# Threshold attention on one core: the last of 48 head pairs taken out of the screen and computed whole in float32

## The chip, the core and the metric

The kernel runs on one core of a Trainium2 chip. The core has a matrix engine (PE, with its weight loads as a row of their own, PEld), a vector engine (DVE), a scalar engine (ACT), a general engine (POOL) and a queue engine for transfers (SP). Each engine works through its own list in order and waits on semaphores. The metric is the device time of one execution in microseconds (us); the time of a kernel is the median of its runs.

## The reference

Q, K and V have 8 batches x 12 heads, each with 512 rows of 64 floats. The threshold is 0.1.

```python
scale = 1.0 / np.sqrt(Q.shape[-1])
scores = np.einsum('bhqd,bhkd->bhqk', Q, K) * scale
weights = np.exp(scores - np.max(scores, axis=-1, keepdims=True))
weights = weights / (np.sum(weights, axis=-1, keepdims=True) + 1e-10)
weights = np.where(weights > threshold, weights, 0)
weights = weights / (np.sum(weights, axis=-1, keepdims=True) + 1e-10)
return np.einsum('bhqk,bhkd->bhqd', weights, V).astype(np.float32)
```

Most rows of random data have no weight above 0.1, and their output is zero. A row with exactly one weight above 0.1 gets that weight normalised to one, so its output is the V row of that key. The kernel relies on this: it finds the few rows that may hold such a weight, computes these exactly, and copies V rows. A check at the end branches to a slow general path if a row falls outside these cases.

## The kernel before, in words

**Tiling.** The 96 heads make 48 pairs (`hp`), two pairs make one of 24 quads (`q`, four heads), eight pairs make one of six groups (`x`). Two heads of a pair lie on the lower and the upper 64 partitions, so that their matmuls use the two row halves of PE.

**The screen, for each pair, in float16.** K is loaded (SP, `load_k`, L399), transposed on PE (`ktr`, L422) and copied out of PSUM in float32 (`kev`, into `kt`); POOL casts it to float16 (`kh`). Q is cast on POOL (`qcast`, L412), transposed (`qtr`, L433) and copied out (`qev`). Four score steps (`sc`, L468) give, for both heads, 128 keys x 512 queries each. ACT or DVE takes the exponential of each (`ex`; ACT at L476, DVE at L478 by an integer trick), and two `g` steps of eight matmuls each (L497) add up sums and high powers of them over the keys into one PSUM bank, `acc`, which holds a whole group. `bits` and `size` (L458, L504) add a bound on the norms of the rows. So `acc` is complete after the last `g` and `size` of a group, and `evac` (DVE, L507) copies it out.

**The exact rows, for each group.** After `evac` come `test` (PE, L513), `flags` (DVE, L517), `rank` (PE, L523 and L525), `key` (DVE, L529), `oh` (a one-hot array, DVE, L533), `idx` (eight matmuls on PE, L543, which turn the one-hot array into row numbers), `idxev` and `base` (DVE, L547 and L552), `gather` (POOL, an indirect DMA of up to 128 rows of Q, 16 slots for each pair, L557), `split` (POOL, L564), `xtr` (PE transpose, L569), `xev` (copy, ACT or DVE), `xqk` (PE, float32 scores of the gathered rows against `kt`, eight matmuls in 32-column tiles, L583), `xexp` (ACT, exponential with the row sum, L589), `xcut` (DVE, threshold times sum, L594), `xkeep` (DVE, which compares and adds up the number of the one key above, L598), `xvi` and `xoi` (DVE, L604 and L609), `gv` (POOL, gather of V rows, L613) and `scatter` (POOL, an indirect DMA of these rows to the output, L620). The output is set to zero beforehand by 24 stores from SP (`z`, L627). For all groups but the last this chain lies beside the screens of the next group. The chain of group 5 has nothing behind it.

**The order.** The order of all 1148 steps is written out by hand in the table `ORDER`: a token is a step's number, the letter of its engine (A, D, G, P, S) and the buffers it takes. `Plan.run` issues the steps in this order, so each engine's list is the table filtered by its letter. Steps are declared with their predecessors by `add`. Two `spare` steps issue matmuls on an idle tile into `acc` (L201): 6 behind `rank` and 17 behind `idx` of group 5. `check` steps gather the conditions for the branch at the end (L733 to L757).

In the table of before, PE's list ends: the last `g` of pairs 45, 46 and 47, with `xtr` of group 4 ahead of the last one, then `xqk` 4, `test` 5, `rank` 5, `spare` 0, `idx` 5, `spare` 1, `xtr` 5, `xqk` 5. DVE's ends: `evac` 5, `flags` 5, `xcut` 4, `xkeep` 4, `xvi` 4, `xoi` 4, `key` 5, `oh` 5, `check` 1, `idxev` 5, `base` 5, `xcut` 5, `xkeep` 5, `xvi` 5, `check` 2, `xoi` 5. POOL's ends: `gv` 4, `gather` 5, `split` 5, `scatter` 4, `gv` 5, `scatter` 5. A scatter declares the output rows from 0 to the end of its group, so the program makes it wait for every earlier write in these rows to land.

Of the kernel before, what the change touches and what calls it, by code (L numbers as in the profile page):

```python
# [13 lines left out]
12S3 13A2 7G 8G 37S 5G 11D 38S 9G 64S2 6G 0G 88S 14G1 15P0.1 1D 18A3 2G 20P2.3 19A 21D 22A 10D 3G 40P4.5  # L14
23P2.6.13 16D9 17A 4G 65S1 41D 42A 26P1.3.12 24A 25D 29P0.5.11 89S 39G 28A 32P2.4.10 27D 115S1 31A 43G 44P3.6
30D 35P 34A 45D 46A 67P1.5 33D 47P0.4.9 68A8 50P3.6.8 69A 61D2 36P 48A 70G2 49D 52A 53P1.2.7 56P0.5.6 66G0 54A
51D 62P 116S0 91P4.6 58A 55D 90G 71P1.3 156S0 92A 59P 72D 93A 73D 95P2.5 57D 94G 74P1.4.5 77P3.6.4 75A 76D 60P
96A 97D 80P0.1.3 78A 79D 83P2.4.2 82A 118P3.5 81D 85A 98P1.6.1 84D 86P 100A 157S2 119D7 87P 120A 117G1 218S3
112D1 101P0.4.0 99A 104P2.6.13 107P3.5.12 103A 102D 113P 121G1 106A 122P1.4 108D 105A 110P 109D 123A 159P0.6
124A 111P 160D6 161A 125P2.3.11 153D0 128P1.5.10 162G0 63S 127A 131P0.4.9 126D 219S1 130A 154P 134P3.6.8 129A  # L20
158G0 259S2 133D 139P2.5.7 132A 135D 137P 140A 142P1.4.6 136D 145P0.3.5 141A 147D 144A 163P2.6 138P 146A 164D
165D 221P3.4 143A 194D2 148P2.5.4 222A5 166P0.6.3 151P 150D 167A 195P 149D 223A 169P1.3.2 172P0.5.1 260S0 168A
170D 224G3 152P 173A 300S1 171D 175P2.4.0 174A 180P1.6.13 220G1 176D 182A 178P 181D 177A 183P0.3.12 186P2.5.11
184A 179P 187D 185A 225P4.6 262P0.1 188A 226D 227A 189P2.3.10 263D4 192P 190A 114S 264D 228P4.5.9 261G0 191A
155S 231P0.6.8 230D 232A 301S2 234P1.2.7 193P 236A 229D 196S 265G2 237P3.5.6 235A 341S0 197D1 242P0.2.5 233A
245P1.4.4 244D 243A 240P 238A 246D 266P2.6 247A 198P0 239D 303P1.3 267D 268A 248P4.5.3 199D 241P 304A3 256D1
254P 305A 297D0 200P 250A 306G1 251P2.6.2 201D 249A 269P1.3.1 202D1 272P0.5.0 271A 257P 298P 252D 273A 203P4
302G1 274D 270A 275P2.3.13 253A 204D2 278P0.1.12 276D 342S1 206G1 279A 307P5.6 205D 277D 258S 283P2.4.11 308A
255P 299S 309D 285A 281P 280D 403S3 284A 286P0.3.10 338D2 289P5.6.9 287A 292P1.4.8 282P 288D 293A 339P 294D 291A
295P 290A 310P0.2.7 344P1.3 312A 311D 313P4.6.6 343G0 296P 345D2 346A 314A 316P2.5.5 315D 319P0.3.4 318A 347G0  # L30
348P1.4 317D 320A 322P 321D 324P5.6.3 207G1 327P0.2.2 404S0 349D 325A 323P 328D 329A 444S2 208P3 350D 330P1.5.1
326A 333P0.2.0 209D1 332D 331A 351P3.4.13 210P6 335A 352D 334A 379D1 353A 380P 336P 211A1 337P 445S2 212D 405G1
213D 354P1.5.12 340S 406P2.3 356A 485S1 357P0.4.11 214D 215D 355A 407D1 360P5.6.10 216G2 358A 363P 408D 361A
410P1.2 359D 362A 365P0.3.9 409G3 366D 367A 368P4.5.8 364P 369A 370D 371P3.6.7 411A 374P0.4.6 372D 377P 412A
446G0 375D 376A 447P1.5 373A 413P2.3.5 441D0 381S 416P0.4.4 448A0 486S1 378P 417D 449A 451P1.6 526S0 415D 418A
419P0.5.3 450G2 414A 382D0 422P3.4.2 421A 420D 442P 424A 425P 452D 453A 427P2.5.1 423D 430P0.4.0 429A 433P1.6.13
428D 217G 383P3 432A 426P 384D 431A 482D2 385P 434A 436P2.5.12 386D 454P0.4.11 437A 387D0 443S 488P1.3 456A
# [74 lines left out]
def kernel(  # L112
# [13 lines left out]
    nc = tc.nc  # L126
    B, H, S, D = Q.shape
# [6 lines left out]
    GP = 8  # L134
# [700 lines left out]
```

## Time and profile before

| | |
|---|---|
| median of 3 runs | 184.74 us (184.69 to 185.29) |
| profiled execution, its own time | 186.93 us |
| its span | 185.2 us |
| busy share of the span: PE, DVE, ACT, POOL | 90%, 85%, 80%, 46% |
| granted PE clock, mean | 0.986 |
| DMA queue of SP (q1) | 37.50 MB, 72.1% of 16 engines' span |

The span runs from the first to the last recorded instruction or transfer. A row of the profile in order of time gives the start in us, the duration in us, the engine, the line of the kernel, the operation, the tiles written and read with their shapes, and the count of like instructions merged into the row; in brackets stands how long the engine had been idle and what released it. Rows of the chain of waits give start, duration and what the chain ran through. Busy shares are averages over the screens, where three engines are full, and the end, where they are not.

### The profile page before, as it was taken

How to read it: one execution, taken by the hardware profiler on the slowest of the kernel's cores; microseconds unless marked ns; L12 is line 12 of the kernel's file. 1: busy time of each engine (PE TensorE's matmuls, PEld its weight loads, DVE VectorE, ACT ScalarE, POOL GpSimd, SP SyncE). 2: the span in 40 equal slices, each digit the busy share in tenths (PEclk: the TensorE clock that was granted, in tenths of full speed). 3: DMA queues.
4: the chain of work that ended last, by engine and by line, in shares of the span. 5: the costliest groups of instructions: out<-in, count | busy, mean ns of one | idle time of the engine just before them, and what ended most of it. 6: DMA issues, size and time to landing. Idle time of an engine off the chain costs nothing.

```text
span 185.2 us, 5894 instructions
## 1 busy us (share of the span) xinstructions
PE 167.5 (90%) x2272; PEld 69.0 (37%) x2272; DVE 157.2 (85%) x337; ACT 148.8 (80%) x305; POOL 85.7 (46%) x130
## 2 busy tenths in 40 slices
PE   7896999999999999999999998999999999998700
PEld 2443444443343354433545334444344243334200
DVE  6897899999979979879898999999999999955040
ACT  2786999998979999989999697999979999930100
POOL 7751626365346573684441934646706504004322
PEclk9999999999999999999999999999999999999995
DMA  5996999999979999969799789999999000000000
GB/s 139 237 253 166 288 256 251 328 264 355 248 159 333 303 284 292 298 145 207 136 378 395 170 224 340 312 287 292 270 274 370 13 1 11 0 0 5 9 2 10
DMA packets 67457, 38.45 MB, mean 208 GB/s; under 512 B 51901, under 2 KB 64257, under 8 KB 67425
## 3 DMA queue, kind: packets, MB, share of 16 engines
q1 hardware_dynamic: 66576, 37.50, 72.1%
q8 instruction: 19, 0.31, 0.8%
q0 software_dynamic: 576, 0.27, 0.7%
q10 hardware_dynamic: 272, 0.26, 0.5%
q14 instruction: 14, 0.11, 0.2%
HBM read 25.56 MB, written 12.78 MB: 207 GB/s over the span
## 4 chain that ended last, share of the span: by engine, by line
PE 51%; DVE 15%; ACT 11%; issue 8%; DMA 6%; SPq 5%; POOL 1%; POOLq 0%; ACTq 0%; DVEq 0%
PE bank L468 17%; PE acc L497 16%; ACT e L476 10%; DVE e L478 6%; PE bank L583 5%; PE bank L422 5%; SPq L399 4%; DMA k<-in_K_dram 3%; PE bank L433 3%; PE acc L504 2%; DVE v L458 2%; DVE kt L390 2%; DVE oh L533 2%; PE bank L543 1%; DMA vr<-in_V_dram,idx 1%
## 5 line engine op out<-in xcount | busy, mean ns | idle before, releaser
L476 ACT ACTIVATE e<-bank 128x512 f16<-128x512 f32 x236 | 122.0, 631 | 7.6 <-PE bank L468 6.4
L478 DVE TENSOR_SCALAR e<-bank 128x512 int16<-128x512 f32 x148 | 93.6, 680 | 1.6 <-PE bank L468 1.4
L468 PE MATMUL bank<-qk 64*128 64x512 f16 x384 | 66.3, 380 | 2.6 <-DVE e L478 0.5
L497 PE MATMUL acc<-e,w_sum 128*32 128x512 f16 x384 | 56.8, 383 | 0.1
L497 PE MATMUL acc<-e,w_pow 128*32 128x512 bf16 x384 | 56.8, 384 | 0.0
L392 POOL CAST qk<-kt 128x1024 f16<-128x1024 f32 (+1 forms) x25 | 25.8, 1034 | 40.5 <-DVE kt L390 24.3
L412 POOL TENSOR_SCALAR qh<-q 128x512 f16<-128x512 f32 x48 | 32.5, 678 | 20.0 <-DMA q<-in_Q_dram 10.2
L468 PEld LDWEIGHTS <-qk 64*128 64x128 f16 x384 | 18.5, 94 | 38.4 <-issue 35.1
L497 PEld LDWEIGHTS <-w_sum 128*32 128x32 f16 x384 | 13.8, 95 | 25.7 <-issue 20.6
L422 PE MATMUL bank<-identity_f,k 64*128 64x64 f32 x384 | 17.6, 229 | 1.7 <-DMA k<-in_K_dram 1.3
L422 PEld LDWEIGHTS bank<-identity_f,k 64*128 64x128 f32 x384 | 14.6, 140 | 8.6 <-issue 3.0
L458 DVE TENSOR_SCALAR v<-qk 128x1024 int32<-128x1024 int32 x24 | 17.1, 720 | 0.7 <-ACT qk L388 0.6
L388 ACT COPY kt<-bank 128x512 f32<-128x512 f32 (+1 forms) x30 | 15.8, 567 | 0.8 <-PE bank L422 0.3
L390 DVE COPY kt<-bank 128x512 f32<-128x512 f32 (+1 forms) x22 | 14.1, 659 | 2.3 <-PE bank L422 2.1
L390 DVE COPY qk<-bank 128x512 f16<-128x512 f16 (+1 forms) x32 | 11.9, 394 | 2.5 <-PE bank L433 2.1
L497 PEld LDWEIGHTS <-w_pow 128*32 128x32 bf16 x384 | 13.8, 95 | 0.3 <-issue 0.2
L613 POOL DMA_INDIRECT vr<-in_V_dram,idx x6 | 6.5, 1081 | 13.8 <-DVE keys L529 8.8
L388 ACT COPY qk<-bank 128x512 f16<-128x512 f16 (+1 forms) x20 | 11.7, 601 | 0.7 <-PE bank L433 0.7
L583 PE MATMUL bank<-kt,xq 128*32 128x512 f32 x96 | 11.5, 598 | 0.4 <-ACT xq L388 0.4
L433 PE MATMUL bank<-identity_h,qh 64*128 64x64 f16 x384 | 10.9, 192 | 0.2
L433 PEld LDWEIGHTS <-qh 64*128 64x128 f16 x384 | 8.6, 95 | 5.9 <-issue 3.8
L201 PE MATMUL acc<-idle 128*128 128x512 f16 x32 | 9.3, 449 | 1.2 <-DVE idle L197 1.2
(94 smaller groups left out, 99.9 us busy)
## 6 DMA issues: line engine op xcount, KB each, us to landing
k<-in_K_dram SPq DMA_DIRECT2D x96, 128.0 KB, 4.8
out_dram<-zero SPq DMA_DIRECT2D x24, 512.0 KB, 6.4
q<-in_Q_dram SPq DMA_DIRECT2D x22, 512.0 KB, 5.7
q<-in_Q_dram SPq DMA_DIRECT2D x3, 256.0 KB, 3.4
q<-in_Q_dram ACTq DMA_DIRECT2D x1, 256.0 KB
qs<-in_Q_dram,idx POOLq DMA_INDIRECT x6, 5.0
vr<-in_V_dram,idx POOLq DMA_INDIRECT x6, 4.0
out_dram<-vr,idx POOLq DMA_INDIRECT x6, 3.8
```

The source lines that it names most:

```text
L388: keep(nc.scalar.copy(dst, src))
L390: keep(nc.vector.tensor_copy(dst, src))
L392: keep(nc.gpsimd.tensor_copy(dst, src))
L412: keep(nc.gpsimd.tensor_scalar(dst, src, ALPHA, 1.0, op0=ALU.mult, op1=ALU.mult))
L422: keep(nc.tensor.matmul(bank_at(("kp", u), i)[:, c:c + D], lhsT=src[ps, n0 + n, r, :], rhs=identity_f32[ps, ps], is_transpose=True, start= ...
L433: keep(nc.tensor.matmul(bank_at(("qp", u), i)[:].bitcast(f16)[:, c:c + D], lhsT=src[ps, n0 + n, r, :], rhs=identity_h[ps, ps], is_transpos ...
L458: keep(nc.vector.tensor_scalar(v_b[at("v", q)][:].rearrange("p a n c -> p (a n c)").bitcast(i32), qk_b[at("qk", q)][:].rearrange("p a n c ...
L468: keep(nc.tensor.matmul(bank_at(("sc", hp, t), h)[:], lhsT=qk[ps, 1, n, t * P:(t + 1) * P], rhs=qk[ps, 0, n, :], start=True, stop=True))
L476: keep(nc.scalar.activation(dst, src, ACTF.Exp, scale=math.log(2.0) / 1024.0, bias=exp_bias))
L478: keep(nc.vector.tensor_scalar(dst.bitcast(i16), src, EXP_BIAS * 1024.0, 0.0, op0=ALU.add, op1=ALU.max))
L497: keep(nc.tensor.matmul(acc[32 * j:32 * j + 32, :], lhsT=w, rhs=rhs, **turn(x, j)))
L583: keep(nc.tensor.matmul(bank_at(("xs", x))[32 * b:32 * b + 32, :], lhsT=xq[:, a * P + 32 * b:a * P + 32 * b + 32], rhs=kt_b[at("kt", GQ * ...
```

## The change

- Pair 47 (`DN`, the last) leaves the screen. The last quad's unit holds one pair; its `bits`, `size` and zero store take half; `acc` of group 5 gets 7 pairs; `limits_last` keeps pair 47's flags at zero; `xqk` 5 has seven matmuls.
- Pair 47 is computed whole. Its K and Q come as one more K-shaped unit (24): both are transposed in float32 and copied out by two `kev` steps. Four `dsc` steps (for 128 queries each, two heads, 512 keys in float32, in PE's two row halves) are followed by eight `dexp` (ACT, with row sum), four `dcut`, eight `dkeep` and four `dvi` (DVE), eight `dgv` (POOL, gathers of 128 V rows each into `d_rows`) and two `dst` (SP, plain stores of 128 KB each, for one head each, behind all four gathers of that head). Rows without a key above the threshold take zeros that `d_rows` was set to.
- `oh` of group 5 becomes two halves, `oh0` and `oh1`, and `idx` two halves of four matmuls, `idx0` and `idx`.
- `spare` becomes three steps of 6 matmuls (behind `rank`, `idx` and the second spare) in place of 6 and 17. A `check` 3 takes in the new pair's conditions.
- The pool of `xe` buffers has 4 in place of 2.
- `ORDER` is written anew from the first line, with 1180 steps. 227 exps of the screen go to ACT and 149 to DVE (236 and 148 before).

The new lists at the end, as the table gives them. PE: `sc` of pair 46 with `dsc` 0 ahead of its last step, `dsc` 1, 3, 2, `size` 23, `g` of 45 (second half), 46, 46, `xtr` 4, `test` 5, `xqk` 4, `rank` 5, `spare` 0, `idx0`, `idx`, `spare` 1, `spare` 2, `xtr` 5, `xqk` 5. ACT: `dexp` (t, h) 0,0, the last `ex` of pair 46, `dexp` 1,0, 1,1, 3,1, 2,0, 2,1, 0,1, 3,0, `xexp` 4, `xev` 5, `xexp` 5. DVE: the last `ex`, `bits` 23, `dcut` 1, `dkeep` 1,0 and 1,1, `dvi` 1, `evac` 5, `xev` 4, `dcut` 2, `dkeep` 2,0, `flags` 5, `dkeep` 2,1, `dvi` 2, `dcut` 0, `dkeep` 0,0, `key` 5, `dcut` 3, `oh0`, `oh1`, `xcut` 4, `check` 1, `idxev` 5, `xkeep` 4, `xoi` 4, `xvi` 4, `base` 5, `dkeep` 3,0, 0,1, `dvi` 0, `dkeep` 3,1, `check` 3, `dvi` 3, `xcut` 5, `xkeep` 5, `xvi` 5, `xoi` 5, `check` 2. POOL: `split` 4, `dgv` 1,1, 1,0, 2,0, 2,1, `gather` 5, `gv` 4, `split` 5, `dgv` 0,0, 0,1, 3,1, 3,0, `gv` 5, `scatter` 4, `scatter` 5. SP: `dst` 1, `dst` 0.

```diff
+    DN = NP - 1
...
     def load_k(u):
...
+            src = (Kf, Qf)[n][DN] if q == NQ else Kf[2 * q + n]
...
-    def do_oh(eng, x):
+    def do_oh(eng, x, cs=slice(0, C2)):
+        k = cs.stop - cs.start
...
+                if GP * x + n == DN:
+                    continue
...
+    def do_dsc(eng, t):
+        kt = kt_b[at("kt", NQ)]
+        for h in range(2):
+            ps = slice(h * D, (h + 1) * D)
+            keep(nc.tensor.matmul(bank_at(("ds", t), h)[:], lhsT=kt[ps, 1, t * P:(t + 1) * P], rhs=kt[ps, 0, :],
+                                  start=True, stop=True))
+
+    def do_dexp(eng, t, h):
+        c = 2 * t + h
+        keep(nc.scalar.activation(xe_b[at("xe", ("d", t, h))][:], bank_at(("ds", t), h)[:], ACTF.Exp, scale=scale,
+                                  accum_out=d_sums[:, c:c + 1]))
+
+    def do_dcut(eng, t):
+        keep(nc.vector.tensor_scalar(d_cuts[:, 2 * t:2 * t + 2], d_sums[:, 2 * t:2 * t + 2], thr, None, op0=ALU.mult))
+
+    def do_dkeep(eng, t, h):
+        c = 2 * t + h
+        keep(nc.vector.scalar_tensor_tensor(out=junk[:], in0=xe_b[at("xe", ("d", t, h))][:], scalar=d_cuts[:, c:c + 1],
+                                            in1=key_no[:].rearrange("p r c -> p (r c)"),
+                                            op0=ALU.is_gt, op1=ALU.mult, accum_out=d_accs[:, c:c + 1]))
...
+    def do_dgv(eng, t, h):
+        c = 2 * t + h
+        keep(nc.gpsimd.indirect_dma_start(
+            out=d_rows[:, h, t, :], out_offset=None, in_=Vr,
+            in_offset=bass.IndirectOffsetOnAxis(ap=d_idx[:, c:c + 1], axis=0),
+            element_offset=(2 * DN + h) * S * D, bounds_check=S - 1, oob_is_err=False))
+
+    def do_dst(eng, h):
+        keep(nc.sync.dma_start(out=Of[DN][:, h, :, :], in_=d_rows[:, h, :, :]))
...
-    add(("spare", 1), "PE", [("idx", last)], lambda e: spare(acc, 17))
+    for i, (n, behind) in enumerate(((6, ("rank", last)), (6, ("idx", last)), (6, ("spare", 1)))):
+        add(("spare", i), "PE", [behind], lambda e, n=n: spare(acc, n))
```

More of the change, by code (lines that the diff above doesn't have):

```diff
@@ L282 @@
     limits = consts.tile([P, 4 * COLS], f32)
+    limits_last = consts.tile([P, 4 * COLS], f32)
     tri_f = consts.tile([P, P], f32)
@@ L501, in do_size @@
         v, row = v_b[at("v", q)], 8 + 2 * m
-        for j in range(4):
+        for j in range(4) if q < NQ - 1 else (0, 2):
             w = w_size[j // 2][:, 31 - row:63 - row]
@@ L647, in free @@
             return [("bk", (name, x))]
-        sums_of = [("g", GP * x + m, half) for m in range(GP) for half in range(2)]
+        sums_of = [("g", GP * x + m, half) for m in range(GP) if GP * x + m != DN for half in range(2)]
         sums_of += [("size", GQ * x + m) for m in range(GQ)]
@@ L660, in exact @@
         stage("gather", "POOL", s("idxev"), do_gather, [("qs", x, 1)])
-        stage("split", "POOL", s("gather", "base"), do_split, [("qb", x, 1)], [("qs", x)])
+        stage("split", "POOL" if x < NX - 1 else "POOL DVE", s("gather", "base"), do_split, [("qb", x, 1)], [("qs", x)])
         stage("xtr", "PE", s("split"), do_xtr, bk("xt"), [("qb", x)])
```

237 lines of the change are left out of this document (147 added, 90 removed).

## The prediction

> **What bounds the kernel now.** I read the windows table first, then the chain of waits, then the rows in order of time behind the last screen. Columns of the windows: stretch, its length, then busy us and count for PE, weight loads, DVE, ACT and POOL, the granted clock, the DMA share.
>
> ```profile
> 140.00:150.00 10.00, 9.87 (x146) 3.67 (x147) 10.00 (x19) 9.98 (x21) 5.50 (x6) 1.00 0.35 136
> 150.00:157.00 7.00, 6.79 (x106) 3.00 (x105) 6.56 (x17) 6.70 (x14) 2.40 (x2) 1.00 0.03 7
> 157.00:163.60 6.60, 6.48 (x75) 2.15 (x76) 5.95 (x10) 5.99 (x13) 0.39 (x1) 1.00 0.00 0
> 163.60:170.00 6.40, 5.30 (x48) 2.29 (x41) 4.08 (x14) 0.69 (x2) 1.04 (x1) 1.00 0.02 4
> 170.00:178.00 8.00, 4.91 (x30) 1.54 (x28) 1.48 (x7) 0.95 (x3) 2.57 (x4) 1.00 0.02 5
> 178.00:185.20 7.20, 0.38 (x2) 0.09 (x2) 0.63 (x4) 0.00 (x0) 1.91 (x2) 0.64 0.04 8
> ```
>
> Up to 163.6 us PE, DVE and ACT are all full: 98, 90 and 91% busy in the third row. From 163.6 on they are mostly free; there the five PE figures contain idle-tile matmuls. The end is a chain of short steps:
>
> ```profile
> 163.60 0.81 DVE L507 TENSOR_SCALAR ev<-acc,root_of 128x512 int32<-128x512 int32 x1 [0.66 <-PE acc L497]
> 165.21 0.34 PE L513 MATMUL bank<-test_w,ev 128*128 128x48 bf16 x4
> 165.59 0.36 DVE L517 TENSOR_TENSOR marks<-bank,limits 128x192 bf16<-128x192 f32 x1 [1.18 <-PE bank L513]
> 166.01 0.19 PE L523 MATMUL bank<-marks,tri 128*128 128x64 bf16 x1 [0.45 <-DVE marks L517]
> 167.30 0.21 DVE L529 TENSOR_TENSOR keys<-bank,marks 128x64 bf16<-128x64 f32 x1
> 167.55 0.71 DVE L533 TENSOR_TENSOR oh<-slot_no,keys 128x1024 f16<-128x1024 bf16 x1
> 169.01 0.22 DVE L547 TENSOR_SCALAR idx<-bank,slot_add 128x1 int32<-128x1 f32 x1 [0.18 <-PE bank L543]
> 170.00 1.00 POOL L557 DMA_INDIRECT qs<-in_Q_dram,idx  x1 [1.42 <-DVE ix L552]
> 172.54 0.39 POOL L564 TENSOR_TENSOR qb<-qs,ix 128x128 f32<-128x128 f32 x1 [1.54 <-DMA qs<-in_Q_dram,idx]
> 172.99 0.33 PE L569 MATMUL bank<-identity_f,qb 128*128 128x128 f32 x1 [0.33 <-POOL qb L564]
> 177.37 0.21 DVE L604 TENSOR_SCALAR idx<-accs,ix 128x1 int32<-128x1 f32 x1
> 177.85 1.04 POOL L613 DMA_INDIRECT vr<-in_V_dram,idx  x1 [3.28 <-DVE oks L739]
> 181.15 1.02 POOL L620 DMA_INDIRECT out_dram<-vr,idx  x1 [2.26 <-DMA vr<-in_V_dram,idx]
> ```
>
> Call E the start of evac of group 5, 163.60. Then the gather of Q rows starts at E+6.40, xtr at E+9.39, the gather of V rows (gv 5) at E+14.25, scatter 5 at E+17.55, and the span ends at 185.20, 4.05 behind scatter 5. So the time is E plus 21.6 us of chain, and the change touches both.
>
> **Part 1: E.** The rows that price one step:
>
> ```profile
> 147.01 0.54 PE bank L468 x4
> 147.55 0.55 PE acc L497 x8
> 163.37 1.91 PE L583 MATMUL bank<-kt,xq 128*32 128x512 f32 x16
> 65.35 0.71 PE bank L422 x16
> 152.07 10.65 ACT L476 ACTIVATE e<-bank 128x512 f16<-128x512 f32 x21
> 158.08 4.87 DVE L478 TENSOR_SCALAR e<-bank 128x512 int16<-128x512 f32 x8
> 165.35 0.60 ACT L589 ACTIVATE xe<-bank 128x512 f32<-128x512 f32 x1 [2.04 <-PE bank L583]
> 165.84 0.19 ACT L589 ACTIVATION_READ_ACCUMULATOR xe<-bank 128x1 f32 x1
> 166.26 0.75 DVE L598 SCALAR_TENSOR_TENSOR junk<-xe,sums,key_no 128x512 bf16<-128x512 f32 x1
> 166.93 0.08 DVE L598 DVE_READ_ACCUMULATOR junk<-xe,sums,key_no 128x1 f32 x1
> 166.07 0.15 DVE L594 TENSOR_SCALAR sums<-sums 128x1 f32<-128x1 f32 x1
> 163.04 0.27 ACT L388 COPY xq<-bank 128x128 f32<-128x128 f32 x1 [0.32 <-PE bank L569]
> 4.95 0.62 POOL L412 TENSOR_SCALAR qh<-q 128x512 f16<-128x512 f32 x1
> 5.20 0.69 PE L422 MATMUL bank<-identity_f,k 64*128 64x64 f32 x8
> ```
>
> A pair's score step (two heads) is 0.27 us on PE, half a g 0.55, a float32 pass over 512 columns in one round of tiles 1.91/4 = 0.48; an exp steps at 10.65/21 = 0.51 on ACT and 4.87/8 = 0.61 on DVE; an exp with row sum 0.49 to its read plus 0.19 = 0.68; a keep 0.67 + 0.08 + a gap = 0.79, a cut or an index step 0.15 to 0.2.
>
> PE, ahead of E: pair 47 loses 4 score steps (1.08) and 2 g (1.10), half a Q transpose and half a size (0.3 together); it gains 8 float32 transposes, half of 0.71 (0.35), and four dsc, all listed ahead of the last g. The trace has no float32 matmul in 64-row tiles. If the two heads run side by side like the 64-row score steps, a dsc is two passes, 0.96, four 3.84; if they run one behind the other, 7.68; less than 3.84 is excluded, since two passes of one head can't overlap on the same rows. I take 3.84, as both tilings in the trace do overlap. Net: -2.48 + 0.35 + 3.84 = +1.7.
>
> ACT, ahead of E: the table has 227 exps for 236, -9 x 0.51 = -4.6; of the six dexp listed ahead of evac only three stand in a chain to it (dexp 0,0 ahead of the last screen exp, and 1,0 and 1,1, which feed dkeep on DVE), +2.0; copies about nought. Net -2.5.
>
> DVE, ahead of E: one exp more (+0.6), two keeps (+1.6), dcut and dvi (+0.3), five half-size K copies for two full ones and shorter Q copies (about 0), a half-size kh (+0.3), half a bits (-0.3). Net +2.5. Note dvi 1 and its keeps are queued ahead of evac: the chain dsc 1 (0.96), two dexp (1.4), dcut, two keeps, dvi (2.0) is 4.4 us behind the last score step; PE needs three dsc, size and three g, 2.9 + 0.2 + 1.65 = 4.75 for the same stretch. So PE, not this new wait, ends last.
>
> The three sums are -2.5, +2.5 and +1.7; exps can move between ACT and DVE, whose mean is 0. PE is the fullest (98%, with 0.12 us idle in 6.6), so its sum weighs most: I take **+1.3**, with -2.5 and +2.5 as ends. POOL's three more memsets (an estimate: 0.5 together) and the new order of its constants lie ahead of the first Q cast, which stood at 4.95; PE's first K transposes come at 5.20 and K's copies behind them, so up to 0.3 of a later cast is covered and I count nothing. The extra K-shaped loads of pair 47's Q replace Q loads of the same bytes, and the DMA share late is 0.03: nothing. The half zero store: nothing.
>
> **Part 2: E to gv 5.** Test now runs ahead of the exact matmuls of group 4 (before, behind them: 0.8 lost), so it ends at E+1.2. But DVE's list reads evac, xev 4, dcut, dkeep, flags: 0.75 + 0.3 (as ACT's copy of xq) + 0.2 + 0.79 puts flags at E+2.0, where it was (E+1.99). Rank now waits behind xqk 4 on PE, which waits for xev 4: E+1.1 plus 1.9 gives E+3.0 to 3.1, before E+2.41. Then dkeep, dvi, dcut, dkeep lie ahead of key: E+4.15, before E+3.70. One-hot in halves lets four of eight index matmuls lie beside the second half, worth 0.3; check 1 sits ahead of idxev. idxev E+5.95, before E+5.41: **+0.5**. POOL has four dgv ahead of this gather; at 1.04 each, the last started behind dvi 2 at E+3.5, they end at E+5.6, no wait. gv 4 (1.04) fits into the 2.5 us in which the gather lands. Behind split 5 (E+9.9) stand four dgv, to E+14.1; gv 5 would be due at E+14.75. They just fit. Ends: 0 if the gather has 0.27 us of lag (gv 5 had: index written by 177.58, start 177.85) for its 0.77 before; +1.3 if the DMA issues don't fit. Fewer spare matmuls leave PE idle about 1.5 us ahead of xtr 5; the clock was 1.00 in the window 170 to 178, with 3 us of idle PE: nothing.
>
> **Part 3: gv 5 to the end.** Scatter 4 moves from ahead of gv 5 to behind it. In the program as it was, each scatter waits for the landing of the one ahead of it, since their declared rows of out overlap; the two dst stores lie in scatter 5's rows too. So scatter 5 gets two new waits.
>
> ```profile
> 177.85 2.50 DMA vr<-in_V_dram,idx
> out_dram<-vr,idx POOLq DMA_INDIRECT x2, 2.2
> vr<-in_V_dram,idx POOLq DMA_INDIRECT x2, 2.4
> k<-in_K_dram SPq DMA_DIRECT2D x96, 128.0 KB, 4.8
> ```
>
> The first row is of the chain, two are of the DMA view from 165 us on, the last is of the page; figures are us to landing. Before: gv 5 landed 2.50 behind its start, and scatter 5 started 0.8 later, at +3.30. Now scatter 4 starts at +1.04, lands at +3.24, and with the same 0.8 scatter 5 starts at +4.05. The last dgv starts at E+13.1, lands at E+15.5; dst 0 lands 2.2 later (as a scatter) to 4.8 later (as a K load under traffic). DMA is all but idle here, so nearer the low end: 2.5, E+18.0, scatter 5 at E+18.8, the same place. **+0.75**, ends +0.75 and +3.0. A write's landing is never free to the next: the Trainium skill, DMA: Bandwidth & Descriptors, section "Anatomy of one DMA — SWDGE (gpsimd) path", puts about 2.0 us of fixed time, mostly the write's receipt, HBM's the slowest, into each DMA, plus bytes over 436 GB/s: as an estimate 2.3 us for the 128 KB of dst, and the sum would be 0.2 less on that branch and unchanged overall.
>
> **The sum.** 1.3 + 0.5 + 0.75 = +2.55. The profiled execution took 186.93 us, 185.20 of span and 1.73 around it; its median of three is 184.74, 2.19 below it. So span 187.75, and a median of 184.74 + 2.55 = **187.3**.
>
> **Rivals.**
> *ACT sets E (faster).* The exps leave ACT, and if DVE absorbs its 2.5 in its 10% of idle and PE likewise, E moves by ACT's -2.5: 184.74 - 2.5 + 1.25 = 183.5. For it: ACT ran 21 exps without a gap to 162.7. Against: PE goes on with the last g until evac at 163.60. It decides from E earlier by 1.8. Chance 0.16.
> *Half of it.* E earlier by about 1.25, given back behind: 184.7. Chance 0.13.
> *POOL becomes the queue.* Indirect DMA instructions are not all 1.04:
>
> ```profile
> 125.94 1.38 POOL L557 DMA_INDIRECT qs<-in_Q_dram,idx  x1 [2.21 <-DVE idx L547]
> 167.54 1.04 POOL L613 DMA_INDIRECT vr<-in_V_dram,idx  x1 [8.79 <-DVE keys L529]
> ```
>
> At 1.38 the four dgv behind split 5 take 1.4 more, of which 0.65 is covered: gv 5 0.8 later, dst with it: 188.1. Against: the second row ran beside the one-hot, a DVE step with two SBUF inputs, in 1.04. Chance 0.12. The Trainium skill, GPSIMD Engine Reference, section "1. Specifications", says that POOL's SBUF interfaces contend with VectorE instructions of two SBUF inputs, which the keeps are; by that rule this case is the likely one, and the second row doesn't bear it out.
> *The store is slow.* dst lands in 4.8: scatter 5 at +3.0 in place of +0.75, 189.5. Chance 0.07.
> *The two heads don't overlap in float32.* +3.84 on PE: 191.1. Chance 0.05.
> The forecast itself, 186.0 to 188.5: 0.47.
>
> From these cases: slower by over 0.3% (0.55 us, about what a measurement here tells from no change) 0.71, within 0.13, faster 0.16. The range leaves out most of the first rival below and the last above: 184.4 to 189.8.
>
> **What would show it.** Right: dsc rounds near 0.48 on PE, evac 5 near 164.9, four dgv in a row between split 5 and gv 5 with little idle, scatter 5 released by a landing of out and not of vr, about 4 us behind gv 5. Wrong: evac ahead of 162; scatter 5 still 3.3 behind gv 5; keeps that delay evac behind the last g; or a new order of the table that gains or loses microseconds in the middle, which no row here can price.

## The result, and the profile after

| | before | after |
|---|---|---|
| median beside each other | 185.01 us (184.69 to 185.66) | 191.48 us (190.06 to 191.69) |
| ratio after/before, 95% interval | | 1.033 [1.027, 1.039] |
| profiled execution, and its span | 186.93, 185.2 us | 191.46, 189.7 us |
| E, start of `evac` 5 | 163.60 | 164.87 |
| `gather` 5, `gv` 5, `scatter` 5 start | E+6.40, +14.25, +17.55 | E+6.38, +15.06, +20.66 |
| end of the span | E+21.6 | E+24.83 |

The change made the kernel slower by 3.3%, more than forecast (187.3, range to 189.8). Medians, ranges and ratios here and below leave out executions more than 1.5% above the quickest of the same kernel. Between the two profiled executions lie 4.53 us, and the places in the table add up to the 4.5 of the spans: E +1.27, E to `gv` 5 +0.81, `gv` 5 to `scatter` 5 +2.30, and +0.12 behind it. The windows of after, cut at its own E (164.87); columns as in the prediction:

```profile
150.00:157.00 7.00, 7.00 (x122) 3.62 (x120) 6.75 (x17) 6.96 (x16) 1.83 (x3) 1.00 0.02 5
157.00:164.87 7.87, 7.87 (x67) 3.36 (x63) 6.62 (x16) 7.18 (x19) 0.22 (x1) 1.00 0.01 2
164.87:171.30 6.43, 5.76 (x49) 2.56 (x50) 6.25 (x25) 2.48 (x8) 4.89 (x5) 1.00 0.02 3
171.30:180.00 8.70, 3.94 (x24) 1.11 (x22) 5.10 (x25) 0.95 (x3) 6.81 (x8) 1.00 0.03 5
```

PE shows no idle time in the 7.87 us up to E. From E to the gather it is DVE that is full (6.25 of 6.43), and then POOL is the busiest (6.81 of 8.70, plus 0.30 of idle time between two transfers in a row). The rows in order of time:

```profile
160.27 2.92 PE L657 MATMUL bank<-kt 64*128 64x512 f32 x12
164.51 0.17 DVE L675 TENSOR_SCALAR d_idx<-d_accs 128x2 int32<-128x2 f32 x1
164.87 0.81 DVE L524 TENSOR_SCALAR ev<-acc,root_of 128x512 int32<-128x512 int32 x1 [0.19 <-PE acc L514]
166.31 1.33 POOL L680 DMA_INDIRECT d_rows<-in_V_dram,d_idx  x1 [0.31 <-issue]
167.88 0.20 PE L540 MATMUL bank<-marks,tri 128*128 128x64 bf16 x1
168.18 1.46 POOL L680 DMA_INDIRECT d_rows<-in_V_dram,d_idx  x1 [0.55 <-DVE d_cuts L666]
168.69 0.22 DVE L546 TENSOR_TENSOR keys<-bank,marks 128x64 bf16<-128x64 f32 x1
169.95 1.00 POOL L680 DMA_INDIRECT d_rows<-in_V_dram,d_idx  x1 [0.30 <-issue]
170.26 0.21 DVE L565 TENSOR_SCALAR idx<-bank,slot_add 128x1 int32<-128x1 f32 x1
170.38 0.74 DVE L619 SCALAR_TENSOR_TENSOR junk<-xe,sums,key_no 128x512 bf16<-128x512 f32 x1
171.25 1.00 POOL L575 DMA_INDIRECT qs<-in_Q_dram,idx  x1 [0.30 <-DVE junk L619]
171.49 0.74 DVE L670 SCALAR_TENSOR_TENSOR junk<-xe,d_cuts,key_no 128x512 bf16<-128x512 f32 x1
172.55 1.34 POOL L634 DMA_INDIRECT vr<-in_V_dram,idx  x1 [0.30 <-DVE junk L670]
174.38 0.33 PE L587 MATMUL bank<-identity_f,qb 128*128 128x128 f32 x1 [1.58 <-POOL qb L582]
174.67 1.03 POOL L680 DMA_INDIRECT d_rows<-in_V_dram,d_idx  x1 [0.35 <-DVE oks L840]
175.06 1.92 PE L603 MATMUL bank<-kt,xq 128*32 128x512 f32 x14 [0.36 <-ACT xq L402]
178.62 1.00 POOL L680 DMA_INDIRECT d_rows<-in_V_dram,d_idx  x1 [0.31 <-issue]
178.79 0.21 DVE L625 TENSOR_SCALAR idx<-accs,ix 128x1 int32<-128x1 f32 x1
179.93 0.99 POOL L634 DMA_INDIRECT vr<-in_V_dram,idx  x1 [0.30 <-DVE oks L832]
181.22 1.02 POOL L641 DMA_INDIRECT out_dram<-vr,idx  x1 [0.30 <-issue]
185.53 0.99 POOL L641 DMA_INDIRECT out_dram<-vr,idx  x1 [3.29 <-DMA out_dram<-vr,idx]
```

Four things stand in them. `evac` 5 waited 0.19 us for PE, and the last DVE step ahead of it (`dvi` 1, written at 164.68) ended only that much earlier: two engines end within 0.2 us of each other ahead of E. The gather had its index at 170.47 and started at 171.25, behind the first four `dgv`. `gv` 5 had its index at 179.00 and started at 179.93, behind the fourth `dgv`. And `scatter` 5 was released by a landing of out, that of `scatter` 4, which is the longest piece of the chain of waits at the end:

```profile
181.22 3.52 DMA out_dram<-vr,idx
184.74 0.03 POOLq L641
184.77 0.55 issue
```

3.52 us, where the same step of before had a landing 2.2 behind its start.

### The profile page after: what moved, and what is told of

Its sections match the earlier page's. It is cut to its first block, busy times and chain, and to the rows that moved or that the text cites. A ratio compares the mean times of both kernels' runs of the same rounds, so it can differ in the third digit from the quotient of the medians.

```text
span 189.7 us, 5942 instructions
## 1 busy us (share of the span) xinstructions
PE 166.3 (88%) x2255; PEld 69.3 (37%) x2255; DVE 167.2 (88%) x374; ACT 150.6 (79%) x310; POOL 94.2 (50%) x140
## 4 chain that ended last, share of the span: by engine, by line
PE 56%; DVE 25%; ACT 7%; issue 5%; POOL 4%; DMA 2%; POOLq 0%; DVEq 0%; ACTq 0%
PE bank L485 16%; PE acc L514 16%; DVE e L495 12%; PE bank L437 5%; PE bank L603 5%; DVE v L477 4%; ACT e L493 4%; PE acc L521 3%; PE acc L205 3%; DVE qk L404 2%; DVE kt L404 2%; PE bank L448 2%; PE bank L657 2%; DMA out_dram<-vr,idx 2%; ACT kt L402 2%
## 5 line engine op out<-in xcount | busy, mean ns | idle before, releaser
L493 ACT ACTIVATE e<-bank 128x512 f16<-128x512 f32 x227 | 119.2, 619 | 7.0 <-PE bank L485 5.7
L495 DVE TENSOR_SCALAR e<-bank 128x512 int16<-128x512 f32 x149 | 95.1, 680 | 2.6 <-PE bank L485 2.1
L485 PE MATMUL bank<-qk 64*128 64x512 f16 x376 | 63.8, 380 | 3.5 <-ACT e L493 1.3
L514 PE MATMUL acc<-e,w_sum 128*32 128x512 f16 x376 | 54.8, 383 | 0.3 <-DVE ev L524 0.3
L514 PE MATMUL acc<-e,w_pow 128*32 128x512 bf16 x376 | 54.4, 383 | 0.0
L427 POOL TENSOR_SCALAR qh<-q 128x512 f16<-128x512 f32 x47 | 31.5, 670 | 15.2 <-issue 4.5
L477 DVE TENSOR_SCALAR v<-qk 128x1024 int32<-128x1024 int32 (+1 forms) x24 | 19.2, 803 | 0.5
L404 DVE COPY kt<-bank 128x512 f32<-128x512 f32 (+1 forms) x25 | 15.1, 609 | 0.7 <-PE bank L437 0.5
L680 POOL DMA_INDIRECT d_rows<-in_V_dram,d_idx x8 | 8.9, 1109 | 10.2 <-DVE d_idx L675 7.7
L575 POOL DMA_INDIRECT qs<-in_Q_dram,idx x6 | 6.5, 1077 | 13.0 <-DVE idx L565 9.6
```

The source lines that it names most:

```text
L404: keep(nc.vector.tensor_copy(dst, src))
L427: keep(nc.gpsimd.tensor_scalar(dst, src, ALPHA, 1.0, op0=ALU.mult, op1=ALU.mult))
L477: keep(nc.vector.tensor_scalar(dst.bitcast(i32), src.bitcast(i32), 2, 0x1FFF1FFF, op0=ALU.logical_shift_right, op1=ALU.bitwise_and))
L485: keep(nc.tensor.matmul(bank_at(("sc", hp, t), h)[:], lhsT=qk[ps, 1, n, t * P:(t + 1) * P], rhs=qk[ps, 0, n, :], start=True, stop=True))
L493: keep(nc.scalar.activation(dst, src, ACTF.Exp, scale=math.log(2.0) / 1024.0, bias=exp_bias))
L495: keep(nc.vector.tensor_scalar(dst.bitcast(i16), src, EXP_BIAS * 1024.0, 0.0, op0=ALU.add, op1=ALU.max))
```

## The experiments

Each was timed beside the kernel before, on the same chip as that; the medians of before there were 185.87 to 186.04.

**The base.** Nothing was edited: before itself.

> The kernel before, unchanged, profiled once more. The first profiled execution of before took 186.93 us (span 185.2), 2.2 us above the median of its runs, while the changed kernel's took its median (191.46, span 189.7). Theory A (the first profile was an odd execution, and the step I priced against it carries its 2 us): this profile has a span near 183.0, and the 2.2 us are missing at one place, so that evac 5 starts near 161.4 in place of 163.6 or the end behind scatter 5 is shorter. Theory B (a profile costs before 2.2 us always): the span is again 185.2 with evac 5 at 163.6.

Measured: 186.43 us against 185.87, ratio 1.0001 [0.9973, 1.003], span 184.7, E at 163.39. Neither expectation met its numbers. What follows: the first profile of before (186.93) was an ordinary execution, near the upper end of these (185.13 to 186.96), and the first median, 184.74 of three runs, was the low end of before. The prediction subtracted the 2.19 between these two from its sum.

**Scatter 4 left out.**

```diff
     def do_scatter(eng, x):
+        if x == NX - 2:
+            return
```

> The changed kernel without the scatter of group 4 (its rows stay zero). Theory A (scatter 5 waits for the landing of scatter 4, which takes 3.5 us because three of its 16 parts land 1.3 us late): scatter 5 then waits for gv 5 (landed 182.3) and dst 0 (182.7) only, starts at 183.4 to 183.6 in place of 185.5, and the time falls by 1.9 to 2.1 us. Theory B (the dst stores, not scatter 4, hold scatter 5): less than 0.4 us.

Measured: 189.46 us, ratio 1.0196 [1.0167, 1.0226]; `gv` 5 at E+15.25, `scatter` 5 at E+18.78, 3.53 behind it. Without the scatter ahead of it, `scatter` 5 is nearly back at the distance of before (3.30 and 3.02 in two profiles), and 2.0 us of after are gone: Theory A. The two `dst` stores stayed. The later one landed at 182.77, 0.31 behind the landing of `gv` 5, and `scatter` 5 came behind it, so here they cost 0.3 us at most.

**The four `dgv` behind `split` 5 left out.**

```diff
     def do_dgv(eng, t, h):
         c = 2 * t + h
+        if t in (0, 3):
+            return
```

> The changed kernel without four of the eight gathers of V rows of pair 47 (t = 0 and 3, those behind split 5; their rows come out zero). Theory A (indirect DMA instructions one behind the other take 1.31 us each and not 1.04, so POOL, not DVE, sets the start of gv 5): gv 5 starts 0.27 behind its index as in the kernel before, 0.65 us earlier, and everything behind it shifts with it, -0.6 to -0.8 us, or -2 if scatter 4's late parts are on time again. Theory B (POOL has slack there): no change of gv 5, and under 0.3 us.

Measured: `gv` 5 at E+14.41 in place of E+15.06, the 0.65 of Theory A; but the median, 191.48 (189.19 to 191.63), ratio 1.033 [1.030, 1.035], did not fall. The profiled execution was the quickest, with `scatter` 4 landing in 2.1 us and `scatter` 5 only 4.35 behind `gv` 5; of the others there is no trace. So the place is as expected, and the gain in time inconclusive: it can be seen only where `scatter` 4 lands on time.

**The branch later.** Eight idle copies on DVE ahead of the reduction whose result the branch waits for.

```diff
+    for _ in range(4):
+        nc.vector.tensor_copy(xe_b[0][:], key_no[:].rearrange("p r c -> p (r c)"))
+        nc.vector.tensor_copy(xe_b[1][:], xe_b[0][:])
+    nc.vector.tensor_scalar(oks[:, 7:8], oks[:, 7:8], xe_b[1][:, 0:1], xe_b[1][:, 0:1],
+                            op0=ALU.subtract, op1=ALU.add)
```

> The changed kernel with eight DVE copies (some 3 us) put ahead of the last matmul of the check, so that the engines branch later. In the trace of the changed kernel, three transfers of the queues called instruction (16 and 8 KB) start 1.8 us after the check's result and run from 182.3 to 183.4 us, over the packets of scatter 4 (182.8 to 183.4), of whose 16 parts three land at 184.7 in place of 183.4. Theory A (code that the branch fetches holds up these three parts, and scatter 5 waits for them): the fetch moves to 185 us or later, scatter 4 lands 2.2 us after its start, scatter 5 starts 1.2 to 1.4 us earlier, and the time falls by about 1.2 us. Theory B (the dst stores or the HBM make scatter 4 late): scatter 4 still takes 3.5 us, and the time is the same or up to 0.5 us longer.

Measured: 190.30 us, ratio 1.023 [1.018, 1.028]; `gv` 5 at E+15.26, `scatter` 4 at E+16.56, landed in 2.16, `scatter` 5 at E+19.51. Adding work took 1.2 us away: Theory A. The DMA view shows the collision. First after between 182.3 and 183.5, then this kernel between 181.5 and 183.6 and between 183.6 and 185.1:

```profile
DMA packets 35, 0.04 MB, mean 33 GB/s; under 512 B 26, under 2 KB 32, under 8 KB 32
q8 instruction: 1, 0.02, 5.7%
q14 instruction: 2, 0.02, 5.3%
q0 software_dynamic: 32, 0.01, 3.3%
```

```profile
q1 hardware_dynamic: 144, 0.13, 18.4%
q0 software_dynamic: 64, 0.01, 3.9%
```

```profile
q14 instruction: 3, 0.02, 4.8%
q8 instruction: 1, 0.02, 4.6%
```

and its chain of waits near the end:

```profile
181.59 2.16 DMA out_dram<-vr,idx
```

The view calls the queues q8 and q14 "instruction"; their packets have 16 KB and 8 KB. In after they run from 182.33 to 183.41, with one more packet to 184.20, about 1.8 us behind the step that writes the branch's result (`over_i`, 180.53), and so just when the 32 packets of `scatter` 4 go out (q0, 182.82 to 183.43). Of the 16 parts of that scatter 13 had landed by 183.38, the last three at 184.69 to 184.74. In the kernel with the late branch the loads came behind the packets, and nothing was late. In before they ran from 180.64 to 182.07, ahead of the packets of `scatter` 5 (from 182.75), and its `scatter` 4 lay 7 us earlier: the order of before kept the two apart. The same can be read in every trace that has `scatter` 4 right behind `gv` 5, some of them of kernels further down:

| trace | packets of `scatter` 4 | loads | landing of `scatter` 4 |
|---|---|---|---|
| after | 182.82 to 183.43 | 182.33 to 184.20 | 3.52 |
| after once more | 184.28 to 184.96 | 184.42 to 185.72 | 4.08 |
| bfloat16 in `dsc` | 183.30 to 184.40 | 182.74 to 185.39 | 3.93 |
| both relieved | 186.50 to 188.22 | 186.59 to 188.21 | 4.37 |
| after without pair 47, first | 183.29 to 184.94 | 183.61 to 184.92 | 4.26 |
| four `dgv` left out | 182.13 to 182.35 | 182.35 to 183.45 | 2.14 |
| the branch later | 183.18 to 183.40 | 183.69 to 184.97 | 2.16 |
| after without pair 47, second | 179.96 to 180.18 | 180.40 to 181.66 | 2.12 |

Where the loads begin ahead of the last packets, one to three parts land late; where the packets are out first, none does. In four of the five late ones the last two packets leave only as the 16 KB packet ends: at 188.18 of 188.21 in "both relieved", where the other 30 had left by 187.14.

The Trainium skill, Runtime: NRT & Kernel Launch, section "Instruction fetch mechanics", says that instructions come in 16 KB blocks by transfers of the engine's own queue, and that a taken branch breaks the sequential prefetch and, where its target is not in the two blocks at hand, forces such a transfer. The 16 KB packet agrees; that it delays parts of another transfer, here by 1.3 us, is from the trace.

**POOL's order: `scatter` 4 well ahead of `gv` 5.**

```diff
-POOL: split 5, dgv 0,0, dgv 0,1, dgv 3,1, dgv 3,0, gv 5, scatter 4, scatter 5
+POOL: split 5, dgv 0,0, scatter 4, dgv 0,1, gv 5, dgv 3,1, dgv 3,0, scatter 5
...
-            out=Or[0:(x + 1) * ROWS, :],
+            out=Or[0:(x + 1) * ROWS - (2 * S if x == NX - 1 else 0), :],
```

> The changed kernel with another order on POOL: behind split 5 come dgv 0,0, scatter 4, dgv 0,1, gv 5, dgv 3,1, dgv 3,0, scatter 5; scatter 5 declares the output rows without pair 47's, so that it doesn't wait for the dst stores. Theory A (POOL's queue of indirect DMAs at 1.31 us each holds gv 5, and scatter 4's landing holds scatter 5): gv 5 starts 14.4 us behind evac 5 in place of 15.06, scatter 5 about 18.3 behind it in place of 20.66 (two dgv of 1.31 lie between, and gv 5's landing), and the time falls by 2.0 to 2.5 us, to about 189. Theory B (the end is set elsewhere, by the dst stores, which now are issued last): less than 1 us.

Measured: 191.09 us, ratio 1.026 [1.021, 1.031]. `gv` 5 at E+14.40 and `scatter` 5 at E+18.30, as Theory A had them, 2.4 earlier than in after; yet the end only at E+23.88, and the time 0.4 less: Theory B for the end. The view of transfers from 183 us on shows what is last:

```profile
184.02 1.02 POOL L639 DMA_INDIRECT out_dram<-vr,idx  x1 [0.30 <-issue]
184.87 1.14 SPq L684 DMA_DIRECT2D out_dram<-d_rows  x2
```

The two `dgv` moved behind `gv` 5 landed late (3.3 and 2.9 us behind their start; their packets lie in the instruction loads of 183.15 to 184.51), so the `dst` stores went out last and landed at 186.4 to 187.4. Pair 47's rows need eight gathers and two stores; whichever way POOL takes them, something is late.

**What sets E: bfloat16 in place of float32 in `dsc`.**

```diff
-            keep(nc.tensor.matmul(..., lhsT=kt[ps, 1, t * P:(t + 1) * P], rhs=kt[ps, 0, :],
+            high = kt[ps, :, :].bitcast(bf16).rearrange("p n (c w) -> p n c w", w=2)[:, :, :, 1]
+            keep(nc.tensor.matmul(..., lhsT=high[:, 1, t * P:(t + 1) * P], rhs=high[:, 0, :],
```

> The changed kernel with the four dsc steps in one pass on the upper halves of the float32 numbers (bfloat16, so pair 47's scores are inexact) in place of float32. Theory A (PE's 4 x 0.97 us of dsc ahead of the last g set evac 5): a step takes 0.27, PE loses 2.8 us, and evac 5 and the time come 1.5 to 2.8 us earlier. Theory B (ACT and DVE, whose exps and keeps stand ahead of evac 5, set it): evac 5 moves by less than 0.7 us.

Measured: 191.54 us, ratio 1.026 [1.020, 1.032]; E at 165.29, 23.07 behind `evac` 4, where after has 23.49 (23.6 in its other profiles). So about 2 us less of matmuls bring 0.4 to 0.6. The DVE rows ahead of `evac`:

```profile
164.42 0.75 DVE L671 SCALAR_TENSOR_TENSOR junk<-xe,d_cuts,key_no 128x512 bf16<-128x512 f32 x1
165.10 0.08 DVE L671 DVE_READ_ACCUMULATOR junk<-xe,d_cuts,key_no 128x1 f32 x1
165.21 0.17 DVE L676 TENSOR_SCALAR d_idx<-d_accs 128x2 int32<-128x2 f32 x1
165.29 0.80 DVE L524 TENSOR_SCALAR ev<-acc,root_of 128x512 int32<-128x512 int32 x1
```

`evac` has no idle time ahead of it: the keeps and `dvi` hold it. Mostly Theory B.

**Both relieved: bfloat16 `dsc`, and the keeps behind `flags` 5.**

```diff
-DVE: bits 23, dcut 1, dkeep 1,0, dkeep 1,1, dvi 1, evac 5, xev 4, dcut 2, dkeep 2,0, flags 5, ...
+DVE: bits 23, evac 5, xev 4, flags 5, dcut 1, dkeep 1,0, dkeep 1,1, dvi 1, dcut 2, dkeep 2,0, ...
```

> The changed kernel with dsc in one bfloat16 pass (pair 47 inexact) and, on DVE, the first cut, two keeps and index step of pair 47 behind flags 5 in place of ahead of evac 5 (two dexp and two dgv move behind them). With dsc alone made cheap, evac 5 came 23.1 us behind evac 4 in place of 23.5, and DVE's keeps ended last. Theory A (PE's dsc and DVE's keeps each set evac 5, within 0.2 us of one another): with both gone evac 5 comes 22.0 to 22.4 us behind evac 4, 1.1 to 1.5 us earlier than in the changed kernel. Theory B (ACT's exps or the new order of the table set it): less than 0.6 us. The end is not expected to gain as much, since POOL's first gathers start 2.5 us later.

Measured: E 22.31 behind `evac` 4, 1.2 less than in after, as Theory A says; and 194.75 us, ratio 1.045 [1.040, 1.050], the slowest of all. The POOL rows:

```profile
168.29 1.05 POOL L679 DMA_INDIRECT d_rows<-in_V_dram,d_idx  x1 [10.19 <-DVE d_idx L674]
172.65 1.00 POOL L679 DMA_INDIRECT d_rows<-in_V_dram,d_idx  x1 [0.30 <-issue]
173.95 1.00 POOL L573 DMA_INDIRECT qs<-in_Q_dram,idx  x1 [0.30 <-issue]
```

The first `dgv` starts at E+3.82, and the gather, queued behind four of them, at E+9.48 in place of E+6.38. The 1.2 us taken off E came back as 3.1 in POOL's queue: the keeps have to lie ahead of `evac`, or their gathers behind the gather of Q. Two more losses in this profile also occur without the new order: `xqk` 5 took 3.55 us at a granted clock of 0.53, where after took 1.92 at 1.00, and `scatter` 4 landed in 4.37.

**What pair 47 costs in the screen.** After with all work of pair 47 left out, once, and once more beside before with the screen steps of pair 47 left out.

```diff
     def do_dsc(eng, t):
+        return
...
```

> The changed kernel with pair 47 left out altogether (no loads, transposes, dsc, dexp, cuts, keeps, index steps, gathers or stores for it; its rows aren't written). It shows what taking a pair out of the screen is worth by itself. Theory A (the screen's 48 pairs take evac 5's 163.4 us evenly, and the tail of the changed order is the one of before): one pair is 163.4/48 = 3.4 us, evac 5 comes near 160.2, and the time is 3 to 4 us below before's, so that pair 47's own work costs the changed kernel about 9 us. Theory B (the new order of the table is itself slower in the middle): evac 5 near 163 and a time within 1 us of before's.

Measured: 187.69 us (187.48 to 189.10), ratio 1.008 [1.004, 1.012]. Still not below before, so Theory A is out; it lies 1.7 above, where Theory B had less than 1. The profiled execution ran at a granted clock of 0.75 in its tail, so its places are not used. The second time:

> The kernel after with all work of pair 47 left out, run once more beside the kernel before with the same work left out. Theory A (the new table loses in its middle): its evac 5 lies at 161.5 to 163, later than that of the other kernel by 1.5 to 2.5 us, and its time is that much longer or more. Theory B (the order is neutral): evac 5 within 0.5 us of the other kernel's, and the remaining difference in time lies in POOL's order at the end, under 1 us.

Measured: 189.63 us (187.27 to 189.71), ratio 1.017 [1.008, 1.026]. And before with

```diff
     def do_sc(eng, hp, t):
+        if hp == NP - 1:
+            return
```

and the same in `do_ex` and `do_g`, with pair 47's flags held at zero as in after:

> The kernel before with its own table, but the score steps, exponentials and g steps of pair 47 left out (its flags kept at zero by the limits of the kernel after; its transposes, size and slots in the last group stay). So its 16 exps come off ACT and DVE (8.8 us of the two together) and 32 score matmuls' and g's worth of 2.2 us off PE, all of them right ahead of evac 5, and nothing else of the order changes. Theory A (the table of after, written anew from its first line, loses about 2 us in its middle): here evac 5 starts 2.5 to 3.5 us earlier than in before, near 160.4, the chain behind it is unchanged, and the time is about 183 us, 2.5 to 3.5 below before. Theory B (one pair less at the end is worth only 1.3 us, whichever order, since something else, the transposes or group 4's steps, keeps PE until then): evac 5 near 162.2, time about 1.2 below before.

Measured: 185.15 us against 186.0, ratio 0.995 [0.993, 0.997]; E at 162.29, 1.1 earlier than in the second profile of before, or 2.0 if counted from `evac` 4 (19.35 us, for 21.3). The tail loses 0.8 of it (gather at E+7.21): `xqk` 4 is now in the way of `test` 5. Theory B, with 0.9 in place of its 1.2. The last pair's steps lie side by side with the rest, so a whole pair less is worth 1 to 2 us, not the 3.3 that a pair takes on average (26.8 us from `evac` 0 to `evac` 1 of before, by eight).

Against this E of after without pair 47, 163.21, is 0.9 later: between the two expectations. Its rows show why:

```profile
161.00 0.42 DVE L484 TENSOR_SCALAR v<-qk 128x512 int32<-128x512 int32 x1
161.48 0.39 PE L528 MATMUL acc<-v,w_size 128*32 128x512 bf16 x2 [1.48 <-DVE v L484]
163.21 0.81 DVE L531 TENSOR_SCALAR ev<-acc,root_of 128x512 int32<-128x512 int32 x1 [1.79 <-PE acc L521]
```

`size` 23 is listed ahead of the last three `g` and waits 1.48 us for `bits`, which DVE does behind its last exponential. In after, the `dsc` fill that time. If nothing else held PE, E would be near 161.7 without that wait (an estimate: 163.21 less 1.48), ahead of the 162.29 of before without pair 47; and its `evac` 4 stood at 141.19, where the other's stood at 142.94. So these two profiles show no loss of the new table in its middle; no run tested it apart. In the profile the kernel still loses 0.9 between `gv` 5 and `scatter` 5 (4.24, for 3.30). In time neither expectation is met: its median lies 4.5 above that of before without pair 47, and the profiled execution, 187.27, was its quickest: what the others lose is not traced.

**After once more.** No edit.

> The changed kernel, unchanged, beside before on this chip. If before's 184.7 us in its first three runs was the low end of its scatter (some twenty later ones of it have medians of 185.9 to 186.1), the ratio is nearer 1.030 than 1.033, and the profile again shows evac 5 at 164.6 to 165.1, gv 5 at evac+15.1, and scatter 5 at evac+20 to 21 or, where the parts land on time, +19.4.

Measured: 191.64 us, ratio 1.029 [1.025, 1.033]. In its profile, an execution of 193.5, E stood at 165.73, and `scatter` 4 took 4.08 to its last landing. `xqk` 5 was slower too. The windows of `xqk` 5, first in after, then here, with the granted clock third from the end:

```profile
175.06:176.98 1.92, 1.92 (x14) 0.40 (x14) 0.00 (x0) 0.00 (x0) 1.62 (x2) 1.00 0.01 0
175.92:179.10 3.18, 3.18 (x14) 0.50 (x14) 0.00 (x0) 0.00 (x0) 2.52 (x3) 0.58 0.02 0
```

Here `gv` 5 waited for its index and not for POOL, and started at E+15.65. Eight traces have after's 18 idle matmuls and 1.58 to 1.63 us of idle PE ahead of `xtr` 5. In three of them the clock fell and `xqk` 5 was late: this one, "`scatter` 4 left out" (2.77 us at 0.67) and "both relieved" (3.55 at 0.53). In the three traces with before's 23 idle matmuls, where that idle time is 0.33, and in three others with 1.00 or 1.21 of it, `xqk` 5 took 1.92 each time. No run gave after its idle matmuls back, so that they are the cause is not shown.

E of after's order thus varies between 164.8 and 165.7 (six profiles with the same lists up to it), against 163.4 to 163.6 of before.

**A version that beats both: before with its tail rearranged.** All 48 pairs stay in the screen. Taken from the change: the one-hot in halves, group 4's steps behind those of group 5, fewer idle matmuls. Added: `xqk` 4 in two rounds, one on either side of `test` and `rank`, and `gather` 5 ahead of `gv` 4.

```diff
-PE:   xtr 4, g, xqk 4, test 5, rank 5, spare (6), idx 5, spare (17)
+PE:   xtr 4, g, xqk 4 (first round), test 5, rank 5, xqk 4 (second round), idx0, idx, spare (14)
-DVE:  evac 5, flags 5, xcut 4, xkeep 4, xvi 4, xoi 4, key 5, oh 5, check 1, idxev 5, base 5
+DVE:  evac 5, flags 5, key 5, oh0, oh1, idxev 5, base 5, xcut 4, xkeep 4, xvi 4, xoi 4, check 1
-POOL: gv 4, gather 5, split 5, scatter 4, gv 5, scatter 5
+POOL: gather 5, gv 4, split 5, scatter 4, gv 5, scatter 5
```

> The kernel before (pair 47 in the screen) with the chain behind evac 5 cleared: the float32 scores of group 4 in two rounds, one ahead of test 5 and one behind rank 5; key, one-hot (in halves, as in the change), idxev and base of group 5 ahead of the keeps and index steps of group 4 on DVE; gather 5 ahead of gv 4 on POOL; 14 idle matmuls in place of 23. Theory A (the end is a chain of steps, in which test lost 0.8 us to PE and key 0.9 us to DVE's steps of group 4): gather 5 at evac+4.7 in place of +6.4, and the whole 1.2 to 1.8 us faster than before. Theory B (the landing of scatter 4 or the branch's code comes to stand last, as in the changed kernel): less than 0.5 us.

Measured: **184.33 us** against 186.0, ratio 0.990 [0.986, 0.993]: 1.0% less, as Theory A has it.

```profile
163.20 0.81 DVE L505 TENSOR_SCALAR ev<-acc,root_of 128x512 int32<-128x512 int32 x1 [0.65 <-PE acc L495]
164.07 0.34 PE L511 MATMUL bank<-test_w,ev 128*128 128x48 bf16 x4
165.26 0.23 DVE L527 TENSOR_TENSOR keys<-bank,marks 128x64 bf16<-128x64 f32 x1 [0.45 <-PE bank L523]
167.90 1.06 POOL L556 DMA_INDIRECT qs<-in_Q_dram,idx  x1 [9.54 <-DVE sums L593]
172.40 1.03 POOL L619 DMA_INDIRECT out_dram<-vr,idx  x1 [1.61 <-DMA vr<-in_V_dram,idx]
175.71 1.04 POOL L612 DMA_INDIRECT vr<-in_V_dram,idx  x1 [2.28 <-DVE oks L753]
```

The gather starts at E+4.70, 1.70 earlier, and the rest of the chain follows as it was: `gv` 5 at E+12.51, the end at E+19.7. `scatter` 4 starts 3.3 us ahead of `gv` 5.

## Why the prediction was wrong, step by step

The direction was right, and so was the wait named in Part 3; its terms were too small, POOL's queue was priced as if it had no gaps, and the base was too low. On the profiled execution's own scale the prediction had +2.55, and +4.53 came: 1.55 missed in Part 3, 0.3 in Part 2, 0.1 behind `scatter` 5. The other 2.19 of the miss come from setting the median at the first three runs' distance below the profile. The later medians of before lie only 0.9 below that profile, so about 1.3 of the 2.19 is a low first median (in the sitting of the result, with 185.01, only 0.3), and the rest is not explained.

**Part 1, E: +1.3 forecast, +1.27 measured** (+1.2 to +2.1 in six profiles). That the two agree so closely is in part luck: +1.3 was a weighing of -2.5, +2.5 and +1.7. The `dsc` came as priced: three take 160.27 to 163.19, 0.97 each, so the two heads overlap, and that rival is out, though its 191.1 lies nearest to the time measured. The claim that PE alone ends last was too simple: DVE's keeps ended 0.19 earlier, and freeing PE alone gave 0.4 to 0.6, freeing both 1.2 or a little more. The rivals in which E moves forward fell with it. ACT had 0.69 of 7.87 us to spare ahead of E, but the dexp, keeps and `dvi` stand in series behind a `dsc`.

**Part 2, E to `gv` 5: +0.5 forecast, +0.81 measured**, by another path. `rank` came at E+3.01, as said; but `key` at E+3.82 and `idxev` at E+5.39 were earlier than forecast (4.15 and 5.95). With the lag of 0.27 the gather was due at E+5.87. It started at E+6.38, since the first step "four `dgv` at 1.04 each, no wait" failed: the last of them ended at E+6.08, not E+5.6, and POOL cost about 0.5 there by these rows. Behind `split` 5 the step "they just fit" failed in the same way. An indirect transfer takes POOL 1.00 to 1.03, but the next one starts 0.30 later, 1.29 to 1.34 from start to start: four take 5.2, not 4.2. The fourth ended at E+14.75, and `gv` 5 was due at E+14.40. The rows of before have no two in succession, so the 1.04 was a duration used as a spacing. The gap could have been read off a row of before in which POOL came straight from another step, and waited for nothing that the profile shows:

```profile
55.12 1.11 POOL L613 DMA_INDIRECT vr<-in_V_dram,idx  x1 [0.28 <-issue]
```

The rival "POOL becomes the queue" was right about the place and about the size of the loss (0.65 of POOL's queue, where it said 0.8), though by this spacing and not by contention: those four ran in 1.00 to 1.03 with DVE nearly idle.

Longer transfers came elsewhere. The `dgv` at 166.31 and 168.18 and `gv` 4 at 172.55, beside the keeps and one-hot steps of DVE, took 1.33, 1.46 and 1.34. The Trainium skill, GPSIMD Engine Reference, section "1. Specifications", names DVE instructions with two SBUF inputs as what contends with POOL, and the keeps are such. These three rows agree with it. The `dgv` at 169.95 and the gather at 171.25 do not: they took 1.00 each, with a keep of 0.74 running beside them from 170.38 and 171.49; nor does a row of before (1.04 beside a one-hot). What else decides, the traces don't say.

The step "fewer spare matmuls: nothing" held in the profiled execution, where `xqk` 5 took 1.92, as in before. In three of eight traces it did not: `xqk` 5 took 2.77 to 3.55 at a granted clock of 0.53 to 0.67. The window that the step rested on, 170 to 178 of before, had only 0.33 us of idle PE right ahead of `xtr` 5; most of its 3 us lay behind `xqk` 5.

**Part 3, `gv` 5 to `scatter` 5: +0.75 forecast, +2.30 measured.** The prediction named the wait (a landing of out, not of `vr`) and mis-sized two of its terms: `scatter` 4 starts 1.29 behind `gv` 5, not 1.04 (the spacing again), and it lands in 3.52, not 2.2. `scatter` 5 follows the landing by 0.79, as said. The 1.3 of the landing is the instruction load of the branch, shown by moving the branch and by the eight traces above. The rival that held +3.0 put it on `dst`: wrong cause, and of the forecasts of this part the nearest in size. `dst` 1 landed at 181.32 and `dst` 0 at 182.68, 1.7 and 1.8 behind their start, where the prediction had 2.5 and, as its other estimate, 2.3; both lay ahead of the late parts of `scatter` 4.

**What stays open.** The medians lie 5.6 us (after once more) to 6.5 us (the result) apart, the profiled executions 4.5, or 5.0 against the second profile of before: 0.6 to 2 us are in no profile. Two things differ between executions of one order, the late parts of `scatter` 4 (2.1 or 3.5 to 4.4 us) and the slow `xqk` 5 (up to 1.6 us more); how often each occurs in executions without a trace is not known. Two packets wait for the 16 KB packet, but their parts land 1.0 to 1.8 us behind the last packet, where 0.3 is usual, and why, the traces don't say.

## What to carry to other kernels

Price a step that is put behind another on a queue engine by the distance from start to start of two such steps in a row, not by the duration of one; where the trace has no two in a row, the idle time between them is an unknown cost with two ends.

Before a write is moved next to the end, look at what else moves bytes there, instruction loads included: a branch near the end has its own transfers, and a wait for a landing takes the slowest of 16 parts. And take a unit of work off a full stage only if its replacement has no serial chain: without the pair's screen E came 1.1 to 2.0 earlier, and with its exact rows 1.3 later than before. So these cost 2.4 or more ahead of E, if the new table is neutral there, and the end lies 3.2 further behind E, the new place of `scatter` 4 included. Last, one trace in which idle time ahead of matmuls costs nothing doesn't make it free: compare the granted clock of several.

## What the runs showed of the hardware

- Two indirect transfers issued in a row by POOL start 1.29 to 1.34 us apart when DVE is nearly idle: 1.00 to 1.03 of work and 0.30 of idle time.
- Beside DVE steps with two SBUF inputs the same instruction took 1.33 to 1.46 three times, and 1.00 twice.
- The load of instructions that follows a branch's result by 1.7 to 2.0 us held up one to three of the 16 parts of an indirect store in all five traces where it began ahead of the last packets: 3.5 to 4.4 us to landing, for 2.1 to 2.2.
- Float32 matmuls of 64 rows in two row halves overlap: 0.97 us for two heads of 128x512.
- In three of eight executions with 1.6 us of idle PE ahead of them, float32 matmuls that take 1.92 us at a granted clock of 1.00 took 2.77 to 3.55 at 0.53 to 0.67.
